# A planner's table of durations, its model of tile forms and of the port that two engines share, and a smaller reserve for matmuls

## The chip, the cores and the metric

The kernel runs on one core of one Trainium2 chip. The metric is the device time of one execution in microseconds. A core has five engines that each work through their own instructions in order: TensorE (PE, with its weight loads shown apart as PEld), VectorE (DVE), ScalarE (ACT), GpSimd (POOL) and SyncE (SP), which here only issues DMAs. An instruction that is not ready blocks everything behind it on its engine.

## The reference, cut to what matters

One decoder block on x of 1 x 512 x 1024 in float32:

```python
xn = rmsnorm(h)                       # attn_pre_norm
z = xn @ w_in                         # 1024 -> 9472 columns, in parts:
#   HGRN2: q, f, i, g (1024 each), 8 heads of 128, chunks of 32
#   RWKV-7: r, k, v (1024 each) and three low-rank parts, 16 heads of 64
#   gates ga, gb (1024 each)
o_a = hgrn2_chunkwise(q, log f, 1 - f, i) -> norm -> * silu(g) -> @ w_branch_a
state = state * w_t + (state a_t) b_t + v_t k_t ; y_t = state r_t      # RWKV-7, 512 steps
o_b = (groupnorm(y) + bonus) * g -> @ w_branch_b
mix = (sigmoid(ga) * y_a + sigmoid(gb) * y_b) @ w_out
h = h + rmsnorm(mix)
u = causal_dwconv3(rmsnorm(h) @ w_up) # 1024 -> 5632
h = h + rmsnorm((silu(gate) * val) @ w_down)
```

## The kernel before, in words

**Split products.** Every large product is made of three float32r matmuls: high by high, high by low, low by high, where a weight block `raw` is copied to `whi_t` by ACT and the rest `wlo_t = raw - whi_t` is made by POOL (in phase 1 in two halves of 128 x 512). One column block of 128 outputs takes 8 x 3 = 24 matmuls of 128 x 512 into a PSUM tile `zps`.

**Phase 1** holds the input product with both token mixers. RWKV-7 runs in chunks of 64 steps. For each of 8 head pairs `hb` there is a *front* (gates, scaled operands, score blocks `sc`), a *solve* (the inverse of a triangular block: many small DVE steps on `nb` and `tmp`, then `Tn`, `fps`, `dps`) and a *chain* (8 chunks one behind the other). A chunk of the chain passes three times from PE to DVE and back: `us` is written by PE, `zs` is copied by DVE, `us` is written from `zs` and `Q`, DVE scales it into `sv`, PE multiplies that with the keys, and DVE adds the old state into the next `sv`. *hgrn* does the other mixer by head. All these generators are woven with the matmuls of `zps`, which fill PE wherever it would wait.

**The planner.** The order of phase 1 is not written out. The class `Plan` takes one operation at a time from each generator. For each waiting operation `prepare` works out when its inputs will be there (the end of the last writer plus a hop between the engines, `HOP`; for a matmul that reads what another engine wrote, `MARGIN` is added as a reserve), `cost` gives its duration, and `run` emits the one that can start first, with ties and small bonuses by kind of work. `emit` notes the planned end. The engines then keep the order in which the planner emitted (`seq`). The planner decides the order alone; on the chip each instruction starts when its semaphores allow. The same class plans the *mix* stage (the product with `w_out`, the norm behind it and the first up blocks).

**Lines.** What the planner emits stands under L207 in the profile of before (the last line of `emit`), and under L229 in the changed kernel; the start of phase 1, which is ordered by hand, stands under L356, and the hand-ordered product `mm3` of the later stages under L321 to L323.

Of the kernel before, what the change touches and what calls it, by code (L numbers as in the profile page):

```python
# [11 lines left out]
ALU = mybir.AluOpType  # L12
# [4 lines left out]
P = 128  # L17
# [25 lines left out]
NWIN = 66  # L43
NX = 2
RAWS = 1
MARGIN = 0.6
AT0 = (3, 2, 4)
XG = ((0, 0),)
MORD = ((0, 0), (1, 0), (2, 0), (3, 0), (0, 1), (1, 1), (2, 1), (3, 1))
# [8 lines left out]
class Op:  # L58
    def __init__(self, key, fn, name, args, kw):
        self.key, self.fn, self.name, self.args, self.kw = key, fn, name, args, kw  # L60
        acc = [a for n, a in kw.items() if n == "accum_out"]
        pos = [a for a in args if isinstance(a, bass.AP)]
        self.outs = pos[:1] + acc
        self.ins = pos[1:] + [a for n, a in kw.items() if isinstance(a, bass.AP) and n != "accum_out"]
        self.bounds = []
        self.ready = None
# [11 lines left out]
class Plan:  # L78
# [8 lines left out]
    def __init__(self, seq, ranks, bonus, at, gaps=False):  # L87
        self.seq, self.ranks, self.bonus, self.gaps = seq, ranks, bonus, gaps
        self.at = dict(zip("TVAGD", at))
        self.dma = 0.0  # L90
        self.wide = True
        self.hist = {}
        self.procs = []
        self.n = 0
        self.now = 0.0
# [33 lines left out]
    def prepare(self, op):  # L129
        t = 0.0  # L130
        for aps, write in ((op.outs, True), (op.ins, False)):
            for ap in aps:
                key, b = self.bound(ap)
                op.bounds.append((key, b, write))
                for c, end, eng, w in self.hist.get(key, ()):
# [4 lines left out]
                    if hit:  # L140
# [3 lines left out]
                        if op.key == "T" and eng != "T":  # L144
                            lag += MARGIN
                        elif eng == "T" and len(op.ins) > 1 and op.ins[1].free_size() == 1:
# [5 lines left out]
    def cost(self, op):  # L152
        out = op.outs[0]
        n = out.free_size()
        scalars = sum(a.free_size() == 1 for a in op.ins) if n > 1 else 0
        far = any(a.space == PSUM for a in op.ins + op.outs)
        if op.key == "T":
            n, m = op.args[2].free_size() if op.name == "matmul" else n, op.args[1].free_size()
            if op.args[1].dtype == F32R:
                op.us = n / 2400 + 0.0022  # L160
            elif op.name == "transpose":
                op.us = 0.109 if n == 128 else 0.055
            elif n == 64 and m == 64:
                op.us = 0.111 if out.offset < 64 * out.ap[0][0] else 0.0535
            elif n == 32:
                op.us = 0.044 if m == 32 else 0.155
            else:
                op.us = 0.218
            op.wide = n > 64 or m > 64
        elif op.key == "V":  # L170
            if op.name == "tensor_reduce":
                n = op.ins[0].free_size()
            rate = 160 if op.name == "reciprocal" else 960
            if op.name in ("tensor_copy", "tensor_scalar", "tensor_single_scalar") and not far:
                rate = 1920
            op.us = 0.069 + n / rate + 0.061 * scalars
        elif op.key == "A":
            op.us = (0.051 if far else 0.093) + n / 1200 + (0.093 if scalars or len(op.outs) > 1 else 0.0)
        elif op.key == "G":
            op.us = 0.147 + n / (470 if op.name == "tensor_tensor" else 840)  # L180
            if op.kw.get("op") == ALU.pow:
                op.us = 0.3 + n * 0.165
        else:
            op.us = 0.475

    def start(self, op):
        return max(op.ready, self.at[op.key])

    def emit(self, op, start):
        end = start + op.us  # L190
        if op.key == "T":
            wide = op.wide
            if wide and not self.wide and start < self.at["T"] + 0.05:
                end += 0.053
            self.wide = wide
        self.at[op.key] = end
        if op.key == "D":
            a = op.outs[0]
            self.dma = max(end + 0.625, self.dma) + math.prod(a.shape) * 4 / 360e3
            end = self.dma + 0.9  # L200
        for key, b, write in op.bounds:
            h = self.hist.setdefault(key, [])
            if write and b is not None:
                h[:] = [e for e in h if not (b[0] <= e[0][0] and e[0][1] <= b[1] and b[2] <= e[0][2]
                                             and e[0][3] <= b[3] and b[4] in (None, e[0][4]))]
            h.append((b, end, op.key, write))
        op.ins_ = self.seq(op.key, op.fn(*op.args, **op.kw))  # L207
# [37 lines left out]
def block_kernel(ctx: ExitStack, tc: tile.TileContext, out: bass.AP, xT: bass.AP, xN: bass.AP,  # L245
# [74 lines left out]
    def mm3(o, lh, ll, rh, rl, start, stop):  # L320
        T.matmul(o, lh, rh, start=start, stop=False)  # L321
        T.matmul(o, lh, rl, start=False, stop=False)  # L322
        T.matmul(o, ll, rh, start=False, stop=stop)  # L323
# [1193 lines left out]
```

## Time and profile before

| what | us |
|---|---|
| median of 3 runs (lowest, highest) | 1255.17 (1254.82, 1256.61) |
| the profiled execution's own time | 1255.5 |
| its span, first to last instruction | 1253.8 |
| PE busy | 1210.6 |
| DVE busy | 732.7 |
| POOL busy | 536.0 |
| ACT busy | 463.6 |

The first product of the stage behind phase 1 (`yps`) starts at 743.7 us; up to 70 us the hand-ordered start runs. PE is busy to 97 per cent of the span. The time of a run is about 1.7 us longer than the span of its profile.

In rows of the timeline the columns are the start, the duration, the engine, the line, the operation, output and inputs by name, the shapes, how many instructions were merged, and in brackets the idle time of the engine before and what ended it. Matmuls are pipelined, so a row's duration is longer than the distance to the next start.

### The profile page before, as it was taken

To read this page: it belongs to the slowest core of one execution; us is meant where nothing else is said; L and a number is where in the kernel's file an instruction comes from. 1 tells how busy PE (TensorE), PEld (TensorE's weight loads), DVE (VectorE), ACT (ScalarE), POOL (GpSimd) and SP (SyncE) were. 2 spreads that over 40 slices of the span, in tenths; PEclk is the share of its full clock that TensorE was granted. 3 is DMA by queue.
4 is the path that set the end of the run, shared out by engine and by line. 5 is a ranking of instruction groups with operands and counts; after the bars stand their busy time and mean duration, and the time that the engine had idled before them with its cause. 6 is when DMAs were issued, how large, how long until landed. Compare 5 with 4: busy or idle time off the path is not lost.

```text
span 1253.8 us, 19765 instructions
## 1 busy us (share of the span) xinstructions
PE 1210.6 (97%) x7748; PEld 949.7 (76%) x7748; DVE 732.7 (58%) x1563; ACT 463.6 (37%) x825; POOL 536.0 (43%) x420
## 2 busy tenths in 40 slices
PE   8889999999999999999999999999999999999997
PEld 6667668667668677686767888888988888888886
DVE  6988887787888988886746304335523232322213
ACT  5533334333343443343332532225534343342321
POOL 6444224342332423242424454432466575565631
PEclk9889899999999999999999999999999999999999
DMA  5121212112112122121221733254323232232332
GB/s 178 50 68 58 65 43 87 49 55 68 50 61 64 54 65 68 43 75 55 70 72 49 240 118 118 86 186 156 130 85 115 90 112 84 84 101 80 122 101 84
DMA packets 54061, 111.01 MB, mean 89 GB/s; under 512 B 21584, under 2 KB 24784, under 8 KB 53968
## 3 DMA queue, kind: packets, MB, share of 16 engines
q1 hardware_dynamic: 53968, 109.75, 27.6%
q8 instruction: 61, 1.00, 0.3%
q14 instruction: 32, 0.26, 0.1%
HBM read 100.29 MB, written 9.44 MB: 88 GB/s over the span
## 4 chain that ended last, share of the span: by engine, by line
PE 75%; DVE 15%; issue 3%; ACT 3%; POOL 2%; DMA 1%; SPq 0%; DVEq 0%; POOLq 0%; ACTq 0%
PE zps L207 20%; PE zps L323 6%; PE zps L322 6%; PE zps L321 6%; PE dn L321 3%; PE dn L323 3%; PE dn L322 3%; PE us L207 3%; PE sc L207 2%; PE yps L321 2%; PE yps L323 2%; PE yps L322 2%; PE vps L207 2%; PE mix L207 2%; DVE X L207 2%
## 5 line engine op out<-in xcount | busy, mean ns | idle before, releaser
L207 POOL TENSOR_TENSOR wlo_t<-raw,whi_t 128x512 fp32r<-128x512 f32 x134 | 184.6, 1397 | 351.3 <-ACT whi_t L207 319.8
L279 POOL TENSOR_TENSOR wlo_t<-raw,whi_t 128x1024 fp32r<-128x1024 f32 x80 | 194.6, 2439 | 96.4 <-ACT whi_t L279 96.2
L207 PE MATMUL zps<-xl,whi_t 128*128 128x512 f32 x488 | 201.3, 413 | 0.0
L207 PE MATMUL zps<-xh,wlo_t 128*128 128x512 f32 x488 | 201.2, 412 | 0.0
L207 PE MATMUL zps<-xh,whi_t 128*128 128x512 f32 x488 | 200.6, 411 | 0.0
L279 ACT CAST whi_t<-raw 128x1024 fp32r<-128x1024 f32 x80 | 83.3, 1049 | 175.5 <-DMA raw<-wup 64.5
L1378 DVE SCALAR_TENSOR_TENSOR u<-zps,pr,u 128x511 f32<-128x511 f32 x40 | 30.0, 750 | 190.7 <-ACT u L1377 190.7
L207 ACT CAST whi_t<-raw 128x1024 fp32r<-128x1024 f32 x71 | 74.4, 1048 | 147.1 <-PE zps L207 68.1
L321 PE MATMUL zps<-x2h,whi_t 128*128 128x512 f32 x320 | 125.5, 392 | 0.0
L323 PE MATMUL zps<-x2h,wlo_t 128*128 128x512 f32 x320 | 125.5, 392 | 0.0
L322 PE MATMUL zps<-x2l,whi_t 128*128 128x512 f32 x320 | 125.5, 392 | 0.0
L207 PEld LDWEIGHTS zps<-xl,whi_t 128*128 128x128 f32 x488 | 92.5, 190 | 20.6 <-issue 0.5
L207 PEld LDWEIGHTS zps<-xh,wlo_t 128*128 128x128 f32 x488 | 92.7, 190 | 20.1 <-issue 0.2
L207 PEld LDWEIGHTS zps<-xh,whi_t 128*128 128x128 f32 x488 | 92.8, 190 | 19.4 <-issue 0.2
L321 PEld LDWEIGHTS zps<-x2h,whi_t 128*128 128x128 f32 x320 | 60.2, 188 | 13.5
L322 PEld LDWEIGHTS zps<-x2l,whi_t 128*128 128x128 f32 x320 | 60.2, 188 | 13.5
L323 PEld LDWEIGHTS zps<-x2h,wlo_t 128*128 128x128 f32 x320 | 60.1, 188 | 13.4
L1403 POOL TENSOR_TENSOR th<-th,u 128x512 f32<-128x512 f32 x22 | 28.4, 1292 | 71.2 <-DVE u L1379 71.2
L207 ACT ACTIVATE sp<-sv,pel 64x64 f32<-64x64 f32 x96 | 33.0, 344 | 67.0 <-DVE sv L207 65.8
L207 PEld LDWEIGHTS us<-sv,X 128*64 128x64 f32 (+1 forms) x480 | 23.8, 134 | 39.7 <-issue 11.6
L207 DVE TENSOR_SCALAR sv<-us,rn 64x64 f32<-64x64 f32 x128 | 35.8, 280 | 29.0 <-PE us L207 25.3
L321 PE MATMUL yps<-oh,whi_t 128*128 128x512 f32 x128 | 50.2, 392 | 0.0
(375 smaller groups left out, 2601.0 us busy)
## 6 DMA issues: line engine op xcount, KB each, us to landing
raw<-win SPq DMA_DIRECT2D x64, 512.0 KB, 3.7
raw<-wup SPq DMA_DIRECT2D x44, 512.0 KB, 3.5
raw<-wdn SPq DMA_DIRECT2D x22, 512.0 KB, 3.5
raw<-wbr SPq DMA_DIRECT2D x16, 512.0 KB, 3.4
raw<-whi SPq DMA_DIRECT2D x8, 512.0 KB, 3.5
raw<-wout SPq DMA_DIRECT2D x8, 512.0 KB, 3.5
xt<-xT SPq DMA_DIRECT2D x8, 256.0 KB, 6.4
oa_d<-hg SPq DMA_DIRECT2D x8, 256.0 KB, 2.2
```

What stands on the lines that cost most here:

```text
L207: op.ins_ = self.seq(op.key, op.fn(*op.args, **op.kw))
L279: return A.copy(hi, raw), eng.tensor_tensor(lo, raw, hi.bitcast(F32), op=ALU.subtract)
L321: T.matmul(o, lh, rh, start=start, stop=False)
L322: T.matmul(o, lh, rl, start=False, stop=False)
L323: T.matmul(o, ll, rh, start=False, stop=stop)
L1378: V.scalar_tensor_tensor(u[:, 1:S], ps[:, 0 : S - 1], pc("cw1", b), u[:, 1:S], op0=ALU.mult, op1=ALU.add)
L1403: G.tensor_tensor(th, th, uv_, op=ALU.mult)
```

## The change

The reserve `MARGIN` falls from 0.6 to 0.45 us. In `cost` a float32r matmul is planned at n/2400 + 0.0165 us instead of n/2400 + 0.0022, one with fewer than 128 rows at 1.86 times that, a DVE scan at n/480 instead of n/960, a DVE read of a 64 x 64 PSUM block 0.07 us longer, an ACT read of 256 columns of PSUM on part of the partitions 0.11 us longer. In `emit` every change of the tile form of PE (rows and columns in use, by 32, 64 or 128) costs 0.1 us and the first full-size matmul after one another 0.1 us; before, only a narrow one followed by a wide one did, 0.053 us. New is `port`: a DVE operation whose operands all lie in SBUF is taken to wait for the end of a POOL operation that is running, and a POOL operation for such a DVE operation.

```diff
-MARGIN = 0.6
+MARGIN = 0.45
...
             if op.args[1].dtype == F32R:
-                op.us = n / 2400 + 0.0022
+                op.us = n / 2400 + (0.0165 if n > 256 else 0.013)
+                if op.args[1].shape[0] < P:
+                    op.us *= 1.86
...
             op.us = 0.069 + n / rate + 0.061 * scalars
+            if op.name == "tensor_tensor_scan":
+                op.us = 0.069 + n / 480
+            if n == 64 and out.shape[0] == 64 and far:
+                op.us += 0.07
+            op.shared = not far and op.name in ("tensor_copy", "tensor_scalar", "tensor_single_scalar", "tensor_tensor",
+                                                "scalar_tensor_tensor", "tensor_tensor_scan")
...
     def start(self, op):
-        return max(op.ready, self.at[op.key])
+        s = max(op.ready, self.at[op.key])
+        other = {"V": "G", "G": "V"}.get(op.key)
+        if other and getattr(op, "shared", True):
+            for a, b in self.port[other]:
+                if a <= s < b:
+                    s = b
+        return s
 
     def emit(self, op, start):
         end = start + op.us
         if op.key == "T":
-            wide = op.wide
-            if wide and not self.wide and start < self.at["T"] + 0.05:
-                end += 0.053
-            self.wide = wide
+            if op.form != self.form:
+                end += 0.1
+            elif self.first and op.form == (P, P):
+                end += 0.1
+            self.first = op.form == (P, P) != self.form
+            self.form = op.form
+        if op.key in self.port and getattr(op, "shared", op.kw.get("op") != ALU.pow):
+            self.port[op.key] = self.port[op.key][-3:] + [(start, end)]
```

No instruction is added or removed: each engine has the same instructions as before, and phase 1 and the mix stage have another order.

**Chain on PE.** The first place is on PE in the chain of the last head pair, between two handoffs to DVE; `us<-sv` hands over to the copy `zs`, and `us<-zs,Q` is what waits for it. Before:

```order
2240 L207 MATMUL us<-sv,X_5744 64x64 x2
2241 L207 MATMUL yp<-sv,X_5744 64x64 x2
2242 L207 MATMUL zps<-xl,whi_t 128x512
2243 L207 MATMUL zps<-xh,wlo_t 128x512
2244 L207 MATMUL zps<-xh,whi_t 128x512
2245 L207 MATMUL zps<-xl,whi_t 128x512
2246 L207 MATMUL zps<-xh,wlo_t 128x512
2247 L207 MATMUL us<-zs,Q 64x64 x2
```

And in the changed kernel:

```order
2194 L229 MATMUL us<-sv,X_5748 64x64 x2
2195 L229 MATMUL yp<-sv,X_5748 64x64 x2
2196 L229 MATMUL zps<-xl,whi_t 128x512
2197 L229 MATMUL zps<-xh,wlo_t 128x512
2198 L229 MATMUL zps<-xh,whi_t 128x512
2199 L229 MATMUL us<-zs,Q 64x64 x2
```

Between the two there are three matmuls of `zps` instead of five.

**Scan on DVE.** The second place is on DVE, also in the chain of the last head pair, where `hgrn` starts its last head with two blocks of `f` and the scan into `p`. Before:

```order
1096 L207 TENSOR_TENSOR sv<-us,sp 64x64 x2
1097 L207 COPY zs<-us 128x64
1098 L207 TENSOR_SCALAR f_122<-hf,fb,fa 128x16x16 x2
1099 L207 SCALAR_TENSOR_TENSOR p_6753<-f_122,r_123 128x544
1100 L207 TENSOR_SCALAR sv<-us,rn_5593 64x64 x2
```

And in the changed kernel:

```order
1107 L229 COPY zs<-us 128x64
1108 L229 TENSOR_SCALAR sv<-us,rn_5659 64x64 x2
1109 L229 TENSOR_REDUCE ym<-yp 128x8
1110 L229 TENSOR_SCALAR ym<-ym 128x8
1111 L229 TENSOR_TENSOR ys<-yp,ym 128x512
1112 L229 TENSOR_SCALAR f_122<-hf,fb,fa 128x16x16 x2
1113 L229 TENSOR_REDUCE yss<-yp 128x8
1114 L229 SCALAR_TENSOR_TENSOR p_6868<-f_122,r_123 128x544
```

The scan and the two blocks ahead of it stood between two steps of the chain and now stand behind its last one.

**First front on DVE.** The third place is on DVE in the front of the first head pair, ahead of the evacuation of the first score block, `X<-sc,mr`. Before:

```order
82 L207 SCALAR_TENSOR_TENSOR hq<-hq,zps 128x512
83 L207 RECIPROCAL r_777<-p_766 128x68
84 L207 TENSOR_TENSOR rkl<-rk,rkh 128x512
85 L207 TENSOR_TENSOR X_727<-sc,mr 64x4x64
86 L207 RECIPROCAL r_777<-p_766 128x68
87 L207 TENSOR_TENSOR X_727<-sc,incl 64x4x64
```

And in the changed kernel:

```order
82 L229 SCALAR_TENSOR_TENSOR hq<-hq,zps 128x512
83 L229 RECIPROCAL r_795<-p_770 128x68 x4
84 L229 TENSOR_TENSOR rkl<-rk,rkh 128x512
85 L229 TENSOR_TENSOR X_714<-sc,mr 64x4x64
86 L229 RECIPROCAL r_795<-p_770 128x68
87 L229 TENSOR_TENSOR X_714<-sc,incl 64x4x64
```

Four blocks of the reciprocal stand ahead of the evacuation instead of one.

More of the change, by code (lines that the diff above doesn't have):

```diff
@@ L90, in __init__ @@
         self.dma = 0.0
-        self.wide = True
+        self.form = (P, P)
+        self.first = False
+        self.port = {"V": [], "G": []}
         self.hist = {}
@@ L168, in cost @@
                 op.us = 0.218
-            op.wide = n > 64 or m > 64
+            op.form = tuple(32 if x <= 32 else 64 if x <= 64 else P for x in (op.args[1].shape[0], m))
         elif op.key == "V":
@@ L176, in cost @@
             op.us = 0.069 + n / rate + 0.061 * scalars
+            if op.name == "tensor_tensor_scan":
[4 more added lines that the diff above has]
+                                                "scalar_tensor_tensor", "tensor_tensor_scan")
         elif op.key == "A":
             op.us = (0.051 if far else 0.093) + n / 1200 + (0.093 if scalars or len(op.outs) > 1 else 0.0)
+            if far and n == 256 and out.shape[0] < P:
+                op.us += 0.11
         elif op.key == "G":
```

## The prediction, as made before the changed kernel ran

> **What bounds the kernel now.** I read the page's first part, then the windows by stage, then the waits of PE in the planned stage, then the timeline around each long wait. PE is the busiest engine by far:
>
> ```profile
> PE 1210.6 (97%) x7748; PEld 949.7 (76%) x7748; DVE 732.7 (58%) x1563; ACT 463.6 (37%) x825; POOL 536.0 (43%) x420
> ```
>
> The windows (stretch, its length, then busy time of PE, PEld, DVE, ACT and POOL, the granted clock, DMA) show where PE has room, and that is what a change of order can win:
>
> ```profile
> 80.00:690.00 610.00, 585.73 (x4904) 436.61 (x4904) 490.14 (x1250) 220.62 (x484) 209.05 (x188) 0.99 0.20 60
> 690.00:744.00 54.00, 54.00 (x234) 43.48 (x233) 11.21 (x10) 24.50 (x31) 26.59 (x19) 1.00 0.55 182
> 800.00:900.00 100.00, 99.15 (x518) 83.91 (x517) 46.73 (x55) 39.41 (x66) 31.60 (x33) 1.00 0.43 148
> ```
>
> From 80 to 690 us PE is idle for 610 - 585.73 = 24.3 us. DVE works 490 of these 610 us, 80 per cent, so it is close behind. From 690 us on PE has nothing to lose. The mix stage, which the planner orders too, lies in the third row, with 0.85 us of idle time in all. So the prize is the 24.3 us. The waits of PE in that window (who waited for whom, us in total, times, longest) say whose they are:
>
> ```profile
> PE us L207 <- DVE sv L207: 5.4, 7, 1.8
> PE fps L207 <- DVE Tn L207: 5.4, 4, 3.0
> PE sc L207 <- DVE X L207: 5.1, 2, 4.8
> PE yt L207 <- DVE ys L207: 2.8, 2, 1.8
> PE us L207 <- DVE zs L207: 2.5, 5, 0.8
> PE vp L207 <- DVE ys L207: 1.7, 1, 1.7
> PE ops L207 <- DVE st L207: 0.6, 1, 0.6
> ```
>
> These seven add to 23.5 us, and DVE ends each. Nearly all the waiting is few and long events, not a steady loss at every handoff.
>
> **Why DVE was late there.** The two longest waits of the chain, at 261 and 653 us:
>
> ```profile
> 257.77 2.88 POOL L207 TENSOR_TENSOR wlo_t<-raw,whi_t 128x512 fp32r<-128x512 f32 x2 [5.61 <-ACT whi_t L207]
> 258.21 1.27 DVE L207 TENSOR_TENSOR tmp<-nb 64x26 f32<-64x26 f32 x1
> 259.51 1.19 DVE L207 TENSOR_TENSOR nb<-nb,tmp 64x26 f32<-64x26 f32 x1
> 261.24 0.34 PE L207 MATMUL us<-sv,X 128*64 128x64 f32 x4 [1.76 <-DVE sv L207]
> ...
> 648.41 2.58 POOL L207 TENSOR_TENSOR wlo_t<-raw,whi_t 128x512 fp32r<-128x512 f32 x2 [5.53 <-ACT whi_t L207]
> 648.86 2.27 DVE L207 TENSOR_SCALAR f<-hf,fb,fa 128x256 f32<-128x256 f32 x2 [0.97 <-ACT hf L207]
> 651.17 1.29 DVE L207 TENSOR_TENSOR_SCAN p<-f,r 128x544 f32<-128x544 f32 x1
> 653.00 0.34 PE L207 MATMUL us<-sv,X 128*64 128x64 f32 x4 [1.58 <-DVE sv L207]
> ```
>
> In each, a DVE instruction with all its operands in SBUF ends with a POOL subtraction that began before it. `tmp<-nb` on a larger block takes far less when POOL is idle, as these two rows show:
>
> ```profile
> 119.39 0.19 DVE L207 TENSOR_TENSOR tmp<-nb 64x36 f32<-64x36 f32 x1
> 118.93 0.20 DVE L207 TENSOR_TENSOR tmp<-nb 64x44 f32<-64x44 f32 x1
> ```
>
> So a held one costs about 1.0 us more, which is more than the room of a chain step. The old table knows neither that nor the scan, which it has at 0.069 + 544/960 = 0.64 us where 1.29 us were measured. Four more waits, each with its bracket:
>
> ```profile
> 284.04 0.66 PE L207 MATMUL fps<-Tn,X 32*32 32x32 f32 x18 [1.00 <-DVE Tn L207]
> 335.68 0.33 PE L207 MATMUL us<-zs,Q 64*64 64x64 f32 x4 [0.78 <-DVE zs L207]
> 354.96 0.66 PE L207 MATMUL vp<-ident,v 128*128 128x128 f32 x4 [1.69 <-DVE ys L207]
> 412.99 0.63 PE L207 MATMUL yt<-ident,ys 128*128 128x128 f32 x4 [1.82 <-DVE ys L207]
> ```
>
> Their causes stand on DVE and POOL just ahead:
>
> ```profile
> 279.46 1.76 DVE L207 SCALAR_TENSOR_TENSOR ys<-ys,lnw,bo 128x512 f32<-128x512 f32 x1
> 333.47 1.29 DVE L207 TENSOR_TENSOR_SCAN p<-f,r 128x544 f32<-128x544 f32 x1
> 352.38 1.67 DVE L207 SCALAR_TENSOR_TENSOR ys<-ys,lnw,bo 128x512 f32<-128x512 f32 x1
> 409.87 2.01 POOL L207 TENSOR_TENSOR yss<-yss,mhalf 128x8 f32<-128x8 f32 x1
> ```
>
> Two held instructions, a scan, and a slow power on POOL, whose cost the change leaves alone. Of these six waits, 1.76 + 1.58 + 1.00 + 0.78 + 1.69 = 6.8 us come from what the new table knows, and 1.8 us do not.
>
> **The change part by part.**
>
> *A. Better knowledge of DVE.* Two waits of the 23.5 us I take out: the longest `sc` wait (4.8) and the longest `fps` wait (3.0) lie at the start of phase 1, where the first head pair has no other chain to hide behind. For `sc` the new order has 24 matmuls of `zps` between the first two score groups instead of 15, nine more:
>
> ```profile
> 301.49 0.39 PE L207 MATMUL zps<-xh,wlo_t 128*128 128x512 f32 x1
> 301.81 0.34 PE L207 MATMUL us<-sv,X 128*64 128x64 f32 x4
> 302.07 0.33 PE L207 MATMUL yp<-sv,X 64*64 64x64 f32 x4
> 302.33 0.50 PE L207 MATMUL zps<-xh,whi_t 128*128 128x512 f32 x1
> 302.67 0.39 PE L207 MATMUL zps<-xl,whi_t 128*128 128x512 f32 x1
> 302.90 0.40 PE L207 MATMUL zps<-xh,wlo_t 128*128 128x512 f32 x1
> 303.13 0.40 PE L207 MATMUL bps<-rkh,blk1r 128*128 128x512 f32 x1
> ```
>
> From start to start a full matmul takes 303.13 - 302.90 = 0.23 us, so nine give 2.1 us of cover. But three RECIPROCALs now stand ahead of the evacuation on DVE, at this price each:
>
> ```profile
> 85.41 0.57 DVE L207 RECIPROCAL r<-p 128x68 f32<-128x68 f32 x1
> 88.35 2.32 DVE L207 RECIPROCAL r<-p 128x68 f32<-128x68 f32 x5
> ```
>
> 2.32 / 5 = 0.46, three are 1.4 us. That leaves 0.7 us, which I count as nothing. There remain 23.5 - 7.8 = 15.7 us. The six waits traced come to 6.8 of 8.6 us that the table now knows; the planner will not find another order for each, so I take two thirds of 15.7: **-10.5 us**. Bounds: 0, and all of it.
>
> *B. Smaller reserve.* Counted over the whole order, the matmuls of 512 columns between the first and the last `us` of the eight chains fall from 691 to 508. There are 176 handoffs between PE and DVE in the chains, so each loses 183 x 0.23 / 176 = 0.24 us of cover. (The new price of a full matmul and of a change of form, both higher, have the same effect as the lower reserve: the planner takes fewer matmuls to fill the same time.) What room a handoff has is seen at this one, where nothing waits:
>
> ```profile
> 299.80 0.33 PE L207 MATMUL us<-zs,Q 64*64 64x64 f32 x4
> 300.25 0.60 DVE L207 TENSOR_SCALAR sv<-us,rn 64x64 f32<-64x64 f32 x2 [0.46 <-PE us L207]
> ```
>
> DVE is done at 300.85, and PE comes for it at 301.81: 0.96 us of room. A DVE instruction of 0.7 us in the way still fits into 0.7 us of room, a held one of 1.7 us fits in neither. So the twelve waits of `us` (7 + 5 in the waits above) would each be 0.24 us longer, 2.9 us, if they stayed, and about as many others just miss. Queued behind a late `us` on PE are the fillers `zps`, for which ACT's evacuation and then the fronts wait; POOL and SP have nothing in that queue. For `fps`, `sc`, `yt` and `vp`, whose cover shrinks as well, I add the same once more as an upper bound. Bounds 0 and 8 us. I take **+4 us**, the middle, since term A takes away part of what would be lengthened.
>
> *C. Tile forms.* The new prices could make the planner switch less. They do not: counted by the rows and columns of each matmul, phase 1 has 663 changes of form before and 664 now, and PE leaves the full form 248 times instead of 241. In the rows above, a full matmul followed by a narrow one takes 301.81 - 301.49 = 0.32 us instead of 0.23, and the first full one after a narrow one 302.67 - 302.33 = 0.34; with the way back about 0.3 us in all for leaving and returning. Seven more are 2 us; 13 fewer changes between two narrow forms, at 0.1 us each, give back 1.3. **+1 us** (bounds 0 and 2).
>
> *D. The mix stage* can win 0.85 us at most, and its order moves by a few matmuls. 0, bounds -0.8 and +1.
>
> PE's own work stays as it is. The chains end earlier in the order of PE, but nothing waits for them: behind the last one the gate products still keep PE busy, as the row from 690 to 744 us shows.
>
> **Sum.** 1255.5 (the profiled execution's own time; its span is 1253.8) - 10.5 + 4 + 1 = 1250.0. The median of the runs shown is 0.3 us below the profiled time, so the forecast is 1249.7 us.
>
> **Rivals.**
>
> *R1, the smaller reserve decides: slower.* The plan's windows of the port lie at planned times; if POOL's subtraction starts a few tenths of a microsecond away from its plan, DVE meets it anyway and is held as at 258 us. Then A gives nothing, and B costs its upper bound of 8: 1255.2 + 8 + 1 = 1264. It decides if the waits of PE in phase 1 come to more than 24 us. For it: the POOL subtraction waits for ACT's copy, 5.6 us idle before it in the row at 257.77, so its start hangs on three other engines. Against it: it starts only once in some 5 us.
>
> [...]
>
> *R2, more is won.* All 15.7 us of A go, and half of the two waits at the start (3.9), with B at 0: 1255.2 - 19.6 + 1 = 1237. Against it: DVE is 80 per cent busy, and someone is in the way at times.
>
> *R3, no difference.* A is won at the handoffs that were late and given back at others, because the work of DVE is the same 490 us and the fillers are the same; A at 5 and B with C at 5: 1255.
>
> **How the numbers follow.** Forecast 0.45, R1 0.25, R2 0.12, R3 0.18. A measurement of this kernel tells a change of about 0.2 per cent, 2.5 us, from none. Faster: forecast and R2, 0.57; same: 0.18; slower: 0.25. The forecast's own range is 1244 to 1253 (A between 7 and 15.7, B between 3 and 5). The range to hold 8 times in 10 reaches into R2 and through most of R1: 1240 to 1263.
>
> **What would show it.** After, the PE idle time between 80 us and the end of the last chain should be about 19 us instead of 24. If A is right, waits of `us` for `sv` with a held DVE instruction or a scan just ahead become rare, and the scan of the last head pair no longer stands ahead of an `sv`. If B is right, the waits left are more and shorter, 0.2 to 0.6 us each. If R1 holds, held DVE instructions of 1.2 us and more are as many as before and stand ahead of chain steps. If PE's busy time outside the waits moves by more than 2 us, C is wrong. The forecast is wrong if the first product of the next stage, now at 743.7 us, starts later than that.

## The result, and the profile after

The changed kernel takes 1269.06 us (median of 4 runs, 1266.09 to 1269.88) against 1255.89 us for the kernel before (4 runs, 1254.82 to 1259.5). The ratio is 1.0096 with a 95% interval of 1.0069 to 1.0122: slower by about 13 us, where 5.5 us less was forecast, and outside the range. The profiled execution took 1269.46 us with a span of 1267.7 us.

The first part of the page, and the windows by stage (columns as in the prediction), of the changed kernel:

```profile
PE 1221.3 (96%) x7748; PEld 955.4 (75%) x7748; DVE 722.9 (57%) x1563; ACT 462.7 (37%) x825; POOL 535.9 (42%) x420
```

```profile
80.00:690.00 610.00, 583.19 (x4800) 431.90 (x4800) 475.28 (x1235) 217.90 (x477) 204.97 (x182) 0.98 0.20 60
690.00:744.00 54.00, 53.82 (x291) 43.24 (x291) 15.45 (x25) 23.50 (x35) 24.11 (x20) 1.00 0.50 168
```

In the same 610 us PE now does 4800 matmuls instead of 4904. Its idle time is 610 - 583.19 = 26.8 us, only 2.5 us more than the 24.3 of before, so idle time does not explain the loss. The first product of the next stage (tile, number, duration in ns, first and last start in us), before and then after:

```profile
L321 PE MATMUL yps<-oh,whi_t x27: 389/392/404, 743.7 to 761.7; 128*128 128x512 f32 x27
```

```profile
L343 PE MATMUL yps<-oh,whi_t x7: 389/389/392, 757.3 to 761.4; 128*128 128x512 f32 x7
```

It starts 13.6 us later, and from there to the last instruction both kernels need the same time (1253.8 - 743.7 = 510.1 us before, 1267.7 - 757.3 = 510.4 after): the whole loss lies in phase 1. The waits of PE after:

```profile
PE us L229 <- DVE zs L229: 6.2, 8, 1.7
PE otp L229 <- DVE on L229: 3.9, 3, 3.3
PE us L229 <- DVE sv L229: 3.9, 5, 1.5
PE sc L229 <- DVE X L229: 3.8, 4, 2.6
...
PE fps L229 <- DVE Tn L229: 1.1, 3, 0.7
```

The waits changed places (`fps` for `Tn` fell from 5.4 to 1.1, `us` for `zs` rose from 2.5 to 6.2, `otp` for `on` from 0.2 to 3.9) and did not become fewer.

**Where the 13.6 us are.** A full matmul is shown as 0.39 us long, but the next one starts 0.23 us after it, so a wait of up to 0.16 us behind it does not appear as idle time at all. I therefore measured every start-to-start distance on PE from 70 us to the first `yps` against the usual one for that pair of forms. The excess, and the time at half clock, in us:

| | before | after |
|---|---|---|
| all waits | 29.0 | 35.4 |
| of these over 0.5 us each | 22.9 | 24.1 |
| of these 0.1 to 0.5 us each | 5.4 | 10.8 |
| time at half the granted clock, up to `yps` | 23.9 | 37.5 |
| of this in stretches that begin after 140 us | 0 | 13.7 |

A straight line through the 15 traces of this study in which no instruction was added or split, start of `yps` = 706.3 + 1.08 x waits + 0.31 x time at half clock, leaves 2.0 us of scatter. By it 6.4 us more of waits cost 6.9 us, and 13.7 us more at half clock cost 4.2 us. The other 2.5 us are there by 70 us already: PE has started 271 matmuls by then instead of 282. Of them 1.8 us stand at the last matmul of the hand-ordered start (42.8 us instead of 41.0), which both kernels have in the same order; over the twenty traces of this study it starts anywhere between 40.9 and 43.3 us, so this part is scatter between runs and not the change. The waits there, before and after:

```profile
PE wps L207 <- ACT zwah L207: 1.5, 1, 1.5
PE zps L356 <- DVE xul L356: 2.0, 3, 1.4
```

```profile
PE wps L229 <- ACT zwah L229: 2.2, 1, 2.2
PE zps L378 <- DVE xul L378: 2.7, 3, 2.1
```

**One place in full.** The timeline after, at the longest wait of a chain (PE, DVE, POOL and ACT rows):

```profile
364.96 0.40 PE L229 MATMUL zps<-xl,whi_t 128*128 128x512 f32 x1
...
365.43 1.05 ACT L229 CAST whi_t<-raw 128x1024 fp32r<-128x1024 f32 x1 [3.32 <-issue]
...
366.57 2.52 POOL L229 TENSOR_TENSOR wlo_t<-raw,whi_t 128x512 fp32r<-128x512 f32 x2 [10.97 <-ACT whi_t L229]
...
366.74 1.19 DVE L229 TENSOR_TENSOR kj<-hk,p 128x64 f32<-128x64 f32 x1
...
367.85 1.31 DVE L229 TENSOR_TENSOR kj<-hk,r 128x64 f32<-128x64 f32 x1
...
369.09 0.21 DVE L229 TENSOR_TENSOR kj<-hk,p 128x64 f32<-128x64 f32 x1
...
369.94 0.22 DVE L229 COPY zs<-us 128x64 f32<-128x64 f32 x1
...
370.21 0.33 PE L229 MATMUL us<-zs,Q 64*64 64x64 f32 x4 [1.71 <-DVE zs L229]
...
371.49 0.63 PE L229 MATMUL zps<-xh,wlo_t 128*128 128x512 f32 x1
...
371.92 0.63 PE L229 MATMUL zps<-xh,whi_t 128*128 128x512 f32 x1
```

Two `kj`, a third of which takes 0.21 us when POOL is done, are held to 1.19 and 1.31 us by the two POOL subtractions; the copy `zs` behind them is late, and PE waits 1.71 us. Then full matmuls start 371.92 - 371.49 = 0.43 us apart instead of 0.23. The two windows of 3.4 us, the one with the wait and the next:

```profile
367.60:371.00 3.40, 1.69 (x11) 1.11 (x10) 3.37 (x7) 0.00 (x0) 1.49 (x2) 1.00 0.46 104
371.00:374.40 3.40, 3.40 (x16) 2.27 (x15) 2.97 (x12) 0.00 (x0) 0.00 (x0) 0.50 0.35 128
```

PE was busy for 1.69 of 3.40 us, and in the next window the granted clock is 0.50. So this wait costs twice: 1.7 us, and then about 1.1 us by the slope of 0.31. That happens three times after 140 us in the changed kernel (at 371, 446 and 542 us) and not once in the trace of before, where two windows were about as empty and the clock stayed full (PE busy for 1.71 of 3.40 us at 352.30 and 1.58 at 410.30). The fourth stretch at half clock, at 146 us, has no wait ahead of it. In the window before it PE was busy all the time, with 55 matmuls, nearly all on 32 or 64 rows:

```profile
142.30:145.70 3.40, 3.40 (x55) 2.68 (x53) 3.32 (x8) 2.89 (x6) 1.07 (x1) 1.00 0.03 5
145.70:149.10 3.40, 3.40 (x10) 2.54 (x11) 2.55 (x6) 1.61 (x5) 2.18 (x3) 0.50 0.28 63
```

All stretches at half clock in these two traces last 3.41 or 6.83 us, so they come in steps of 3.41 us. How empty the window ahead was is not the whole condition: of the windows ahead of the stretches at 371 and 146 us one was half busy (1.69 of 3.40 us) and one wholly busy (3.40 of 3.40).

The longest wait of all after 70 us, 3.31 us for `otp` at 126 us, is of the same kind. Two DVE instructions that take 0.68 and 0.73 us at the shortest in this trace are held to 1.77 and 1.74 us beside two POOL subtractions, and the `on` behind them is late:

```profile
121.57 3.11 POOL L229 TENSOR_TENSOR wlo_t<-raw,whi_t 128x512 fp32r<-128x512 f32 x2 [1.17 <-ACT whi_t L229]
121.79 1.77 DVE L229 SCALAR_TENSOR_TENSOR kka<-ta,k 128x512 f32<-128x512 f32 x1
123.48 1.74 DVE L229 SCALAR_TENSOR_TENSOR X<-k,nkk,E 64x512 f32<-64x512 f32 x1
126.00 1.11 PE L229 MATMUL otp<-ident,on 128*128 128x128 f32 x4 [3.31 <-DVE on L229]
```

**Why the held instructions were not planned away.** The planner's own times for this place, beside the measured starts (DVE and PE run 75.7 to 76.2 us behind the plan here, so a difference of 76 means as planned):

```
                                     planned start   measured start   difference
PE   last zps that reads whi_t_3483      289.00          364.96          75.96
ACT  whi_t_3720 (same buffer)            285.92          365.43          79.51
POOL wlo_t, first half                   287.03          366.57          79.54
DVE  kj<-hk,p                            290.44          366.74          76.30
DVE  kj<-hk,r                            290.71          367.85          77.14
```

`whi_t` has two buffers, and this copy writes the one that `whi_t_3483` had. The plan starts the copy 3.1 us before the last matmul that still reads the old block. It can, because `bound` keys the history of `whi_t` by its full name with the number (the set `RING`), so the old block and the new one in the same buffer are strangers; `splits` waits until the matmul has been emitted, but not until its planned time. On the chip the copy waits, and POOL behind it. The bracket of the copy's row names nothing that it waited for; it starts 0.07 us after the end of that matmul (364.96 + 0.40). Of all copies from 80 to 700 us the profile puts the most waiting to `zps` (for 29.5 us in 12 waits it names nothing):

```profile
ACT whi_t L229 <- PE zps L229: 91.3, 24, 7.6
```

So the planned window of the port, 287.03 to 289.50, was over before the `kj`, and the real one lay right on them. Over all of phase 1, 53 of the 65 copies after the first two are planned ahead of the end of the matmul that frees their buffer. Those planned over 0.3 us too early come 3.5 us late (median); those planned no earlier than that end come 0.1 us late; the correlation of the two over the 65 is 0.95. The POOL subtraction begins 1.9 us late in the median, longer than it lasts (two take 2.52 us in the row above), and within 0.3 us of its planned place in 9 of 65 blocks. The error was there before the change too (51 of 65). What the port model did is seen from the held DVE instructions (those over 0.4 us above their planned duration, starting in a real window): before, 25 of 59 began inside that window in the plan too; after, 2 of 51. The planner moved them out of windows that were in the wrong place, and nearly as many others fell into the real ones. (Counted over all traces, with 0.3 us or more over the median of the same instruction, an order made with the port model has 48 to 57 held DVE instructions in phase 1, one made without it 58 to 69. So the model avoids about one in six, not all.)

### The profile page after: what moved, and what is told of

The parts are those of the page before. It is cut to its first block, busy times and chain, and to the rows that moved or that the text cites. A ratio compares the mean times of both kernels' runs of the same rounds, so it can differ in the third digit from the quotient of the medians.

```text
span 1267.7 us, 19777 instructions
## 1 busy us (share of the span) xinstructions
PE 1221.3 (96%) x7748; PEld 955.4 (75%) x7748; DVE 722.9 (57%) x1563; ACT 462.7 (37%) x825; POOL 535.9 (42%) x420
## 3 DMA queue, kind: packets, MB, share of 16 engines
q1 hardware_dynamic: 53968, 109.75, 27.3%
## 5 line engine op out<-in xcount | busy, mean ns | idle before, releaser
L229 POOL TENSOR_TENSOR wlo_t<-raw,whi_t 128x512 fp32r<-128x512 f32 x134 | 181.9, 1378 | 345.3 <-ACT whi_t L229 328.6
L229 PE MATMUL zps<-xl,whi_t 128*128 128x512 f32 x488 | 204.5, 419 | 0.0
L229 PEld LDWEIGHTS us<-sv,X 128*64 128x64 f32 (+1 forms) x480 | 24.0, 135 | 40.9 <-issue 15.8
L345 PE MATMUL yps<-oh,wlo_t 128*128 128x512 f32 x128 | 50.2, 392 | 0.0
```

## The experiments

All edits are in the planner's numbers and lines, except two kinds that keep an order and are described where they come. The code is cut at `...`, and a comment behind `#` in it says which kernel is meant; it is not in the code. Cover means the matmul time between a handoff of the chain to DVE and the matmul that waits for it, the mean over the eight chains: 1.72 us before, 1.38 after. The theories, as the expectations number them: the cover decides (1); the new durations and the port model themselves give a worse order (2); the half clock after 150 us is chance (3); each order is a draw, and a small edit of any number throws it anew (4); part of the loss is the half clock after a window with little PE work (5); A brought what was forecast, and the new PE prices took it back (6). "Ratio" is to the kernel before on the same chip, whose median was 1257.9 to 1259.3 us in these batches.

**The reserve alone, in both planners.**

```diff
-MARGIN = 0.45      # of the changed kernel: 0.6, 0.75, 0.9
+MARGIN = 0.6
-MARGIN = 0.6       # of the kernel before
+MARGIN = 0.45
```

> The changed kernel with the old reserve of 0.6 us; nothing else differs. Theory 1 (too little cover at the handoffs from DVE to PE costs the time): counted in the order, PE work per chain handoff is 1.38 us with the change, 1.72 us before and 1.52 us here, so about 40 per cent of the loss of 13 us comes back: 1262 to 1265 us, and the waits of 0.1 to 0.5 us fall from 10.8 us towards 8. Theory 2 (the new table of durations and the port model themselves give a worse order): no better than 1267 us. Theory 3 (the half-clock windows after 150 us are chance): 3 of them or none, without tie to the waits.

> The changed kernel with a reserve of 0.75 us. PE work per chain handoff is 1.66 us, nearly that of before. Theory 1: 1256 to 1260 us, waits of 0.1 to 0.5 us near the 5.4 us of before. Theory 2: 1265 us or more.

> The changed kernel with a reserve of 0.9 us. PE work per chain handoff is 1.78 us, more than before (1.72). Theory 1 together with the gain that was forecast for the better knowledge of DVE: 1245 to 1252 us. Theory 1 without that gain: 1253 to 1257 us. Theory 2: 1262 us or more.

> The kernel before with the reserve of 0.45 us alone. PE work per chain handoff is 1.54 us, as with the new table and 0.6. Theory 1: 1260 to 1264 us, as slow as the new table at the same cover. Theory 2: 1255 to 1258 us, since the old table is kept.

| | cover | median us | ratio (95%) | waits 0.1 to 0.5 us | waits over 0.5 us | half clock that begins after 140 us |
|---|---|---|---|---|---|---|
| new, 0.60 | 1.52 | 1264.68 | 1.0052 (1.0035-1.0070) | 10.7 | 18.9 | 20.5 |
| new, 0.75 | 1.66 | 1273.06 | 1.0118 (1.0099-1.0138) | 9.3 | 31.0 | 23.9 |
| new, 0.90 | 1.78 | 1269.39 | 1.0081 (1.0054-1.0107) | 8.9 | 24.9 | 34.1 |
| old, 0.45 | 1.54 | 1278.54 | 1.0152 (1.0121-1.0183) | 7.8 | 32.9 | 34.1 |

If the cover decided, the changed planner with 0.90, which has more cover (1.78) than before (1.72), would have been as fast as before. It is 0.8% slower. Theory 1 falls. At 0.60 the time is what theory 1 had (1262 to 1265), but its short waits are not (10.7, where they were to fall towards 8). The old planner at 0.45 is slower than either theory allowed, so theory 2 does not explain these four runs either. But the column of the short waits orders itself: with the new PE prices 8.9 to 10.8 at any reserve, with the old ones 5.4 and 7.8.

**The smallest step of the reserve.** The same line with 0.59 and 0.61 in the kernel before, and 0.44 and 0.46 in the changed one.

> The kernel before with a reserve of 0.59 us instead of 0.60; the table is the old one. PE work per chain handoff is 1.69 us (1.72 before), but after the first 227 matmuls the order is another. Theory 4 (each order is one draw, and the order of before is a good one among its neighbours): 1262 to 1275 us, with half-clock windows behind 150 us that the profile of before does not have. Theory 1 (the cover decides): within 2 us of before.

> The kernel before with a reserve of 0.61 us; PE work per chain handoff 1.75 us. Theory 4: 1262 to 1275 us, several us away from the run with 0.59. Theory 1: within 2 us of before.

> The changed kernel with a reserve of 0.44 us instead of 0.45; PE work per chain handoff 1.39 us (1.38). Theory 4: anywhere from 1258 to 1278 us, with the change of a hundredth of a microsecond moving it by 3 us or more. Theory 1: within 2 us of the changed kernel, so some 10 to 12 us above before.

> The changed kernel with a reserve of 0.46 us; PE work per chain handoff 1.43 us. Theory 4: anywhere from 1258 to 1278 us. Theory 1: within 2 us of the changed kernel.

| | median us | ratio (95%) | all waits | half clock that begins after 140 us |
|---|---|---|---|---|
| old, 0.59 | 1270.82 | 1.0103 (1.0061-1.0144) | 29.8 | 27.3 |
| old, 0.61 | 1257.14 | 0.9987 (0.9972-1.0001) | 27.6 | 3.4 |
| new, 0.44 | 1277.17 | 1.0117 (1.0070-1.0164) | 41.2 | 41.0 |
| new, 0.46 | 1263.05 | 1.0033 (1.0016-1.0050) | 30.7 | 6.8 |

One hundredth of a microsecond of reserve costs up to 13 us (0.60 to 0.59 in the old planner) and wins up to 8 us (0.45 to 0.46 in the changed one). So the loss of 13 us is no larger than the spread among neighbours of one planner, and theory 4 holds in the main: the order before is one of the better draws of its planner. The run with 0.61 was not what theory 4 had (1262 to 1275 us); it stayed within 2 us of before. Between 0.59 and before the waits hardly differ (29.8 and 29.0). Of the 16.4 us by which `yps` starts later with 0.59 the slope of 0.31 gives 9.5 us to the clock and the waits about 1; the rest the straight line does not explain. The longest stretch in the kernel with 0.44, windows:

```profile
546.50:577.20 30.70, 25.02 (x197) 21.52 (x195) 18.55 (x30) 5.75 (x20) 7.07 (x7) 0.51 0.07 21
```

**The same order without the long idle windows.** Zero matmuls were put into the waits of PE: 94 in the order of the changed kernel, 90 in that of before. They add nothing to an open `zps`, and every other instruction stays where it was; one copy that makes the zeros is added.

```diff
+        if op.key == "T":
+            if self.fill and self.open is not None:
+                for _ in range(FILL.get(self.tn, 0)):
+                    self.seq("T", self.fill(self.open))
+            self.tn += 1
...
+    plan.fill = lambda ps: T.matmul(ps[0:112], zz, xh[:, 0], start=False, stop=False)
```

> The changed kernel in its own order, with 94 matmuls of 128x112x512 by a block of zeros added on PE, ahead of the matmuls for which PE waited 0.4 us or more in its profile, and as many as fit into each wait (one takes 0.23 us). They add exact zeros to an open product. Theory 5 (the clock is halved after a stretch in which PE does little, and that costs several us): the half-clock windows at 371, 446 and 542 us are gone and some of those before 150 us, and the time falls by 3 to 8 us, to 1260 to 1265. Rival (half-clock windows are chance, or have another cause): as many windows, and the time rises by what of the 94 x 0.23 = 21 us does not fit into a wait: 1269 us or more.

> The kernel before in its own order, with 90 matmuls by zeros added in the same way, ahead of the matmuls for which PE waited 0.4 us or more in the profile of before. Theory 5: the two half-clock windows of 6.8 us at 86 and 134 us are gone or shorter, and the time falls by 2 to 7 us below before. Rival: the same time as before or some us more.

The changed order with them takes 1260.43 us, ratio 1.0020 (1.0007 to 1.0034): 0.8% faster than without them (1.0096), although 94 x 0.23 = 21.6 us of matmuls were added. The same place as above in its trace, timeline and windows:

```profile
360.38 2.53 POOL L240 TENSOR_TENSOR wlo_t<-raw,whi_t 128x512 fp32r<-128x512 f32 x2 [10.94 <-ACT whi_t L240]
...
360.56 1.18 DVE L240 TENSOR_TENSOR kj<-hk,p 128x64 f32<-128x64 f32 x1
...
361.66 1.32 DVE L240 TENSOR_TENSOR kj<-hk,r 128x64 f32<-128x64 f32 x1
...
362.17 1.79 PE L667 MATMUL zps<-xh,zz 128*112 128x512 f32 x7
...
364.03 0.33 PE L240 MATMUL us<-zs,Q 64*64 64x64 f32 x4
```

```profile
361.40:364.80 3.40, 3.33 (x18) 2.33 (x17) 3.37 (x7) 0.00 (x0) 1.51 (x2) 1.00 0.26 75
364.80:368.20 3.40, 3.40 (x28) 2.28 (x28) 3.26 (x12) 0.59 (x1) 0.00 (x0) 1.00 0.51 161
```

The holds are the same (1.18 and 1.32 us), `us` comes 3.65 us after POOL's start, as it did without the zero matmuls (3.64), but the wait is filled and the next window keeps the full clock. This is theory 5, shown in one order. The order of before won nothing from it: 1261.42 us, 1.0020 (1.0001 to 1.0039). The trace of before had no half clock after 140 us to lose, and 90 matmuls that do not fit exactly cost something. And filling the waits does not keep the clock up by itself. The trace of this run, the slowest of its twelve, has two stretches at half clock that the trace of before does not have, 23.9 us in all. The second follows a window in which PE never waited, but 58 of its 60 matmuls had 32 or 64 rows:

```profile
427.10:430.50 3.40, 3.40 (x60) 2.71 (x61) 3.34 (x3) 0.73 (x2) 2.56 (x3) 1.00 0.28 107
430.50:444.20 13.70, 13.70 (x66) 9.82 (x63) 8.49 (x19) 3.84 (x8) 2.18 (x2) 0.50 0.08 26
```

**One part at a time.** First the prices and forms of PE alone in the kernel before (reserve 0.60), and the changed kernel without the port (reserve 0.60).

```diff
-                op.us = n / 2400 + 0.0022        # the kernel before, with the PE lines of the change alone
+                op.us = n / 2400 + (0.0165 if n > 256 else 0.013)
...
-        if other and getattr(op, "shared", True):        # the changed kernel at 0.6, without the port
+        if False and other and getattr(op, "shared", True):
```

> The kernel before with the new prices of PE alone (full matmuls, tile forms), reserve 0.6. PE work per chain handoff is 1.46 us. Theory 4 (each order is one draw): anywhere from 1256 to 1278 us. Of the waits: if the new PE prices make the waits of 0.1 to 0.5 us that the new table shows at every reserve (8.9 to 11.3 us in all; the old table 5.4 to 7.8), they come to 9 us or more here; if the port model makes them, to 8 us or less.

> The changed kernel without the port model and with a reserve of 0.6 us. PE work per chain handoff is 1.54 us. Theory 4: anywhere from 1256 to 1278 us. The waits of 0.1 to 0.5 us come to 8 us or less if the port model makes them, to 9 us or more if the other prices do. If the port model kept DVE from being held, its held instructions (0.3 us or more over their usual time) would be clearly more here than the 53 of the changed kernel; if it does not, as many.

The PE prices alone: 1318.98 us, 1.0481 (1.0448 to 1.0515), cover 1.46 at the unchanged reserve of 0.60, waits of 65.3 us and 71.7 us of half clock after 140 us. The change without the port at 0.60: 1289.65 us, 1.0238 (1.0210 to 1.0267), against 1.0052 with it; that is one pair of orders, and shows no more than that the port model did no harm there. Their windows, the PE prices alone first:

```profile
80.00:690.00 610.00, 561.80 (x4503) 414.12 (x4501) 460.38 (x1164) 203.65 (x446) 182.70 (x164) 0.93 0.18 54
```

```profile
80.00:690.00 610.00, 568.47 (x4714) 418.11 (x4713) 468.05 (x1205) 214.72 (x469) 196.01 (x177) 0.98 0.19 58
```

Both lie above the 1256 to 1278 us that theory 4 allowed, so more than a draw is at work. The short waits follow the PE prices and not the port: counted outside the half clock they come to 5 us before, 10 with the PE prices alone, 9 without the port and 10 in the changed kernel. So the new prices of PE look like the harmful part. Why they cost 61 us here and 13 with the rest of the change is not shown: the cover of 1.46 is more than the changed kernel's 1.38. That looks like theory 6, so its other half was run: the DVE and ACT prices and the port, with PE's old prices.

```diff
+            if op.name == "tensor_tensor_scan":        # the kernel before, with the lines of DVE, ACT and the port alone
+                op.us = 0.069 + n / 480
...
+        other = {"V": "G", "G": "V"}.get(op.key)
```

> The kernel before with term A alone: the new durations of DVE and ACT and the port model, the old prices of PE, reserve 0.60. PE work per chain handoff 1.70 us (1.72 before). Theory 6 (A is worth what was forecast, and the PE prices took it away): 1243 to 1252 us, long waits (over 0.5 us) at 14 us or less instead of 22.9, none of them behind a held DVE instruction of a chain. Theory 4 (one draw, A worth nothing): 1256 to 1272 us, long waits 19 to 29 us.

> The same with a reserve of 0.61: another order of the same kind, PE work per chain handoff 1.72 us. Theory 6: 1243 to 1252 us again. Theory 4: some us away from the run with 0.60, on either side.

> The changed kernel with the old prices of PE: term A with the reserve of 0.45. PE work per chain handoff 1.63 us (1.38 with the change). Theory 6 together with the cover: 1248 to 1258 us, below the old table at the same reserve (1.0152 times before) by 1.5 per cent. Theory 4: 1260 to 1280 us.

At reserves of 0.60, 0.61 and 0.45: 1271.12 us, 1.0095 (1.0064 to 1.0127); 1286.67 us, 1.0216 (1.0194 to 1.0238); 1275.96 us, 1.0129 (1.0101 to 1.0157). A alone is slower than before in three draws of three, and theory 6 falls. Against the old planner at the same reserve it is slower at 0.60 and 0.61 and no slower at 0.45 (1.0129 and 1.0152, with intervals that overlap). Short waits are few again (4.8, 5.5 and 6.9 us), all waits are 28.9, 36.2 and 29.7 us as in other orders, and the time goes to the clock (64.9, 78.5 and 54.6 us of half clock after 140 us). At 0.60, one window of narrow chain work and what follows it:

```profile
604.00:607.50 3.50, 0.63 (x16) 0.36 (x9) 3.46 (x11) 0.27 (x1) 0.00 (x0) 1.00 0.00 0
608.10:645.60 37.50, 32.98 (x230) 24.56 (x230) 28.16 (x94) 8.70 (x25) 6.35 (x6) 0.51 0.15 47
```

**The disputed cost itself, without a new order.** Each POOL subtraction of 128 x 512 in the plan of before is issued as two of 128 x 256, so that a DVE instruction is held by a short one. The order of everything else is that of before. Beside it, two kernels with zero matmuls: 67 in the order of before at 0.61, 65 in the changed one at 0.46.

```diff
+        if op.key == "G" and "wlo_t" in op.outs[0].tensor.name and op.outs[0].free_size() == 512:
+            for c in (slice(0, 256), slice(256, 512)):
+                op.ins_ = self.seq("G", op.fn(*[x[:, c] for x in op.args], **op.kw))
+            return
         op.ins_ = self.seq(op.key, op.fn(*op.args, **op.kw))
```

> The kernel before in its own order on PE, DVE and ACT; each of POOL's subtractions of 128x512 in phase 1 is issued as two of 128x256, so a held DVE instruction could come in between. If the holds make the long waits: waits of PE over 0.5 us fall from 22.9 us to 15 or less, and the time by 4 to 8 us, to 1250 to 1254. If they do not: long waits 20 us or more, and the time the same as before within 3 us (POOL has 0.15 us more work for each of some 110 pieces and room for it).

> The kernel before with a reserve of 0.61, in the order of that run, with 67 matmuls by zeros ahead of the matmuls that waited 0.7 us or more, for 0.8 of each wait. If filling takes out its half-clock windows (10.2 us at 84, 3.4 at 330): 1250 to 1254 us. If the order of before showed the rule (its filling won nothing): 1255 to 1261 us.

> The changed kernel with a reserve of 0.46, in the order of that run, with 65 matmuls by zeros ahead of the matmuls that waited 0.4 us or more, for 0.8 of each wait. If filling takes out its half-clock windows behind 80 us (20.5 us in all): 1254 to 1259 us. If not: 1262 us or more.

The halved subtractions take 1244.51 us, 0.9877 (0.9858 to 0.9896): faster than both kernels, and by more than the 4 to 8 us expected. POOL pays for it. Its group of subtractions in phase 1 (count, total us, mean ns), before and here:

```profile
L207 POOL TENSOR_TENSOR wlo_t<-raw,whi_t 128x512 fp32r<-128x512 f32 x134 | 184.6, 1397 | 351.3 <-ACT whi_t L207 319.8 <-issue 13.6 <-PE us L207 9.3
```

```profile
L209 POOL TENSOR_TENSOR wlo_t<-raw,whi_t 128x256 fp32r<-128x256 f32 x268 | 220.2, 852 | 316.2 <-ACT whi_t L211 279.5 <-PE us L211 15.0 <-issue 13.4
```

It works 35.6 us more, 0.27 us for each of the 134. PE waits for POOL no more than before (1.1 us, in the start). The place that the prediction showed at 257.77 us, in this kernel, and four of its waits of PE from 80 to 700 us:

```profile
255.34 3.05 POOL L209 TENSOR_TENSOR wlo_t<-raw,whi_t 128x256 fp32r<-128x256 f32 x4 [5.26 <-PE us L211]
...
255.65 0.72 DVE L211 TENSOR_TENSOR tmp<-nb 64x26 f32<-64x26 f32 x1
...
256.40 0.66 DVE L211 TENSOR_TENSOR nb<-nb,tmp 64x26 f32<-64x26 f32 x1
...
257.60 0.34 PE L211 MATMUL us<-sv,X 128*64 128x64 f32 x4 [0.64 <-DVE sv L211]
```

```profile
PE sc L211 <- DVE X L211: 5.1, 2, 4.5
PE fps L211 <- DVE Tn L211: 2.9, 4, 1.4
PE us L211 <- DVE zs L211: 2.4, 5, 0.9
PE us L211 <- DVE sv L211: 2.0, 4, 0.9
```

The two held instructions take 0.72 and 0.66 us instead of 1.27 and 1.19, and `us` waits 0.64 instead of 1.76. Waits over 0.5 us fall from 22.9 to 14.8 us, all of them from 29.0 to 21.1, and `yps` starts at 734.0 instead of 743.7. So the holds do cause a good part of the long waits, as step A had it; what failed is the plan's way of avoiding them.

The zero matmuls bring the order at 0.61 to 1253.23 us, 0.9946 (0.9930 to 0.9962; without them 0.9987), and the changed order at 0.46 to 1257.85 us, 0.9992 (0.9977 to 1.0008; without them 1.0033). With the first two this is a gain of about 0.4% twice and of 0.8% once, and a loss of 0.2% in the order of before.

## Why the prediction was wrong

**Step A failed, and with it the sign.** The prediction said "the planner will not find another order for each, so I take two thirds of 15.7: -10.5 us". The waits over 0.5 us rose by 1.2 us instead, the held DVE instructions (0.3 us and more over the usual) are 53 where there were 60, and the part alone is 1.0 to 2.2% slower than before. The reading of the trace was right, since halving the holds in an unchanged order took 7.9 us of waits away. Wrong was the step from "the new table knows it" to "the order avoids it". By the estimate in R1 the plan needs the start of POOL's subtraction to a few tenths of a microsecond, and it has it wrong by 1.9 us in the median. The trace of before held this already in the row at 257.77, which the prediction quoted: POOL waits 5.6 us for ACT's copy. What the copy itself waits for was not asked. The two waits that A left out as fixed, 4.8 us for `sc` and 3.0 us for `fps`, were the ones that shrank (to 2.6 and 0.7 us at the longest), while a wait of 3.3 us for `otp` is new. One reading was loose: of the two rows given for an idle POOL the one at 118.93 ran beside a power on POOL (from 117.98 for 1.10 us) and was not held by it.

**R1 was this mechanism, and had a chance of 0.25.** Its price was 1264 us, 5 us too little; the half clock (4.2 us) stood in no term of it. Its condition was over 24 us of waits (26.8 us of idle time measured) and as many held instructions as before (53 for 60). The rows at 366.57 to 367.85 show it: POOL's two subtractions began first, and the two `kj`, held to 1.19 and 1.31 us, ended about when they did (the second `kj` at 369.16 us, the second subtraction at 369.09). The prediction gave R1 as its ground that POOL's start hangs on three other engines. The runs show a plainer one: the plan lets the copy start before its buffer is free.

**Step B was near in size and only in part right in cause.** +4 us was forecast, as more and shorter waits; the waits of 0.1 to 0.5 us rose by 5.4 us. But they are there at every reserve with the new PE prices (8.9 to 11.3 us) and at none with the old (4.8 to 7.8, at 0.45 too). What the prediction put in brackets, that the new prices of a full matmul and of a change of form act like a lower reserve, is the larger part: at 0.60 they come to 5.4 us with the old prices and 10.7 with the new. The reserve itself adds 2.4 us in the old planner (0.60 to 0.45) and 1.9 in the changed one (0.90 to 0.45). The cover fell by 0.34 us per handoff where 0.24 was worked out from the full matmuls alone.

**Step C and D.** The number of changes of form was counted from the order (664 for 663), and its +1 us is below what the runs could show by itself. Its test by PE's busy time was a bad one: busy time rose by 10.7 us, but it contains the half clock and the short waits that hide in a matmul's shown end. D was right: from the first `yps` to the last instruction both kernels take 510 us.

**What no step had.** The half clock (4.2 us by the straight line; removing it and filling the waits gave back 0.8% in the same order), and 2.5 us before 70 us, of which 1.8 are scatter between runs. The larger miss is that an order is one draw. The prediction summed local gains for an order in which 0.01 us of one number moves the time by anything from 2 to 15 us, and six reserves of the changed planner lie between 1263 and 1277 us, four of the old one between 1256 and 1279. A range that only adds up local bounds is too narrow for such a change.

**Left open.** No kernel was run in which the plan lets the copy wait for its buffer. Whether A would then bring its 10 us is not shown. Nor is it shown why the PE prices alone cost 61 us.

## What to carry to other kernels

Before trusting a planner that avoids a conflict, compare its planned starts with the measured ones for the instruction that causes the conflict: a model like `port` was worth little here, where the other engine's start was off by 1.9 us in the median and its instruction is 1.26 us long (2.52 / 2). A price that is too low can act as a reserve: at the same 0.60 the cover fell from 1.72 to 1.52 us with the corrected prices. But putting the cover back (0.90, 1.78 us) did not bring the time back here. Where a small change of any number throws a new order, compare several neighbours of both planners before crediting the change, and look first for a fix that leaves the order alone, such as shortening the instruction that blocks.

## What the runs showed of the hardware that was not expected

In the traces of both kernels the granted clock of PE falls to half (0.50) for 3.41 or 6.83 us, on a grid that is fixed within a run: in the changed kernel such a stretch begins at 16.01 us and another at 370.99, 104 steps of 3.413 us later. It lies elsewhere in the next run: in the kernel before the first begins at 45.08 us, 8.5 steps after 16.01. It falls also after windows in which PE was far from idle (1.69 of 3.40 us busy at 367.60 and 3.40 of 3.40 at 142.30 in the changed kernel). Counted on that grid from 70 us to the first `yps`, the twenty traces have 3796 windows at full clock, and 91 of them were followed by half clock: all 31 in which PE was busy for less than 0.4 of the window, 38 of the 101 between 0.4 and 0.7, and 22 of the other 3664. In each of these 22 no more than five of the matmuls were full ones of 512 columns, where 3.41 us hold some 15 of them (3.41 / 0.23). That narrow matmuls keep the clock up less than full ones fits these counts; no run here tests it alone.

Once at half, the clock can stay there for 30 us and more (a mean of 0.51 over 30.7 us at 546.50 with the reserve of 0.44, and over 37.5 us at 608.10 with A alone at 0.60). The same kernel varies with it: over 80 runs of the kernel before, from 1254.9 to 1264.3 us (an 81st, of 2842.72 us, is not among them), the time falls by 7.5 us for each 0.01 of mean granted clock (correlation -0.78). The slope of 0.31 gives nearly the same: 0.01 of 1256 us is 25 us at half clock, and 25 x 0.31 = 7.8 us. That it is the place of the grid that makes the runs differ is not shown.
